# The last stage of a hybrid encoder: row factors of blocks 0 to 4 made two blocks later, and block 6's operand traced behind the first projection of block 7

## The chip, the cores and the metric

The kernel runs on one core of a Trainium2 chip. The metric is the device time of one execution in microseconds (us). A core has five engines that run side by side and meet through semaphores: TensorE (PE, matmuls; PEld is its weight load), VectorE (DVE), ScalarE (ACT), GpSimd (POOL) and SyncE (SP). Here nearly all DMAs are issued from SP's queue, one after the other.

## The reference

One layer of an encoder over 2048 + 256 rows of width 1024, in float32. The normalised input is projected once (`u @ w_in`), and the columns feed two mixers that run in both directions over the rows: gated linear attention with 4 heads (the GLA heads) and a Mamba-2 scan with 16 heads in 4 groups (the SSD groups). The outputs of both are normalised, joined and projected, and an embedding is added through a gate:

```
o   = rmsnorm(gla_forward + gla_backward, gla_onorm_g) * silu(z_gla)      # per head of 256
y   = rmsnorm((ssd_forward + ssd_backward + d*x) * silu(z_ssd), ssd_norm_g)
h   = x + concat(o, y) @ w_out
h   = h + sigmoid(h @ w_ple_gate) * rmsnorm(p @ w_ple_proj, ple_norm_g)
out = rmsnorm(h, final_norm_g)
```

The RMS norm of `o` needs one factor for each row and head: rsqrt of the mean of the squares over 256 columns.

## The kernel before, in words

The rows are cut into nine blocks of 256 (`NB = 9`, `T = 256`; block 8 is the second sequence). Everything is held with features on the partitions. Each float32 matmul is made of three in a rounded format: every operand is split into a high part (a copy by ACT, line 130) and a low part (a subtraction, line 126), and lines 195 to 197 multiply high by high, high by low and low by high.

**Stages.** Eight sections follow each other, a GLA head and an SSD group in turn (`s0` to `s7`). Each section walks over all blocks, odd ones from block 8 down to 0, projects, and runs the scan of one direction (`gla_first`, `ssd_first`, and their second halves, which wait in the list `queue`). The scan of the other direction (`second`, line 752) needs the section's stored updates and runs one section later, block by block; the list `carry` holds it until the next projection has been traced (`carried`), and `behind` then takes one entry out of `queue`. `second` ends in `emit`, which writes the gated output to `mixD` and, for a GLA head, the sums of squares of the rows to `ssD`.

**The last stage**, `output` (line 1243), begins when section 7 has been traced. Its first loop goes over the blocks from 8 down to 0 and multiplies the GLA half of `w_out`: four projections `foa` a block, 48 matmuls each, whose results are added to `x` (tile `fx`, line 1259) and stored. The other direction of section 7 runs inside this loop: at the end of each block the gate of the next `second` is made (`fz0zz` is the gate of block 0, `s7b0lo` the output tile of its `second`, and so on upwards), and it runs behind the first projection of the next block. The names of section 7's block 0, such as `s7b0fS`, `s7b0fU`, `s7b0fxh`, `s7b0y`, belong to its forward pass, which still runs while block 8 and 7 are multiplied; `s7b0lpf` is the first matmul group of its `second`, and `s7b0le`, `s7b1le` are row factors of `second` that SP loads (line 642).

**The operand of a block.** `gla_mix(b)` makes the operand of block b, called `fa8m` to `fa0m`: it loads the row factors `r` of the four heads from `rD[b]` (lines 818 to 821, four DMAs that copy one row to all partitions), loads `mixD[b]`, multiplies both on DVE (line 836) and splits the product (ACT, POOL). `fa6r` are the row factors of block 6. Two of the four pieces are made when `gla_mix` is called, the other two by `rest()`. The row factors of several blocks are made together by `gla_rstd` (line 840): it loads the sums of squares from `ssD`, takes Ln and Exp on ACT, and stores the result to `rD`. A call inside section 7 (`f1`) does blocks 5 to 8; the call in `output` (`f0`, tile `f0rc`) does blocks 0 to 4.

**What sets the order.** The code is traced in the order in which it is written, and a scheduler then places each engine's instructions by readiness and traced order; the order on every engine is fixed when the kernel is built. `tc.keep_in_program_order(i)` pins an instruction behind the one traced before it on its engine. A tile taken with `tmp(tag, ...)` gets one of the few buffers of its tag, and waits until one is free:

```python
bufs = {"t4k": 2, "dk": 6, "tm": 2, "zo": 4, "eb": 2, "mx": 7, ...}
r  = [tmp("zo", [P, 2, T], f"{nm}r{j}") for j in range(2)]      # gla_mix: row factors
zz = tmp("zo", [P, 2, T], nm + "zz")                            # gate_z: the gate
o  = tmp("zo", [P, 2, T], nm + "o")                             # second: its output
```

Of the kernel before, what the change touches and what calls it, by code (L numbers as in the profile page):

```python
# [19 lines left out]
NB = NBP + NBS  # L20
# [13 lines left out]
def hybrid(ctx, tc, xT, pT, wsec, wsmall, wlast, wproj, wgate, bgate, norm_g, gla_g,  # L34
# [89 lines left out]
    def split(raw, hi, lo, hi_eng, lo_eng):  # L124
        copy(hi_eng, hi, raw)
        lo_eng.tensor_tensor(lo, raw, hi.bitcast(F32), ALU.subtract)
# [58 lines left out]
    def load_u(b, name):  # L185
        def piece(n, hi, lo):
            for q, t in enumerate((hi, lo)):
                sy.dma_start(t.bitcast(F32), uD[b][n, q])
        return Operand(name, piece)
# [45 lines left out]
    def proj_f(w, u, name):  # L235

        ps = bank("pj", [P, 2, T], name)
        mm3_bank(ps, lambda f: wcols(w, f), lambda f: ucols(u))
        return ps
# [7 lines left out]
    def rstd(ss, r, n, e, pin=False):  # L247

        ln = sc.activation(r, ss, AF.Ln, bias=e[:, 0:1], scale=1.0 / n)  # L249
        if pin:  # L250
            tc.keep_in_program_order(ln)
        sc.activation(r, r, AF.Exp, scale=-0.5)  # L252
# [5 lines left out]
    with ExitStack() as mctx:  # L258
# [6 lines left out]
        def tmp(tag, shape, name, dt=F32):  # L265
            return mp.tile(shape, dt, name=name, tag=tag, bufs=bufs[tag])
# [142 lines left out]
        def carried(ps):  # L409

            while carry:
                carry.pop()()
            return ps

        def behind(n):

            if n:
                queue.pop(0)()
                if len(queue) > QMAX:
                    queue.pop(0)()  # L420
# [389 lines left out]
        def gate_z(pz, nm):  # L810

            zz = tmp("zo", [P, 2, T], nm + "zz")
            sc.activation(zz, pz, AF.Tanh, scale=0.5)  # L813
            ve.scalar_tensor_tensor(zz, zz, 1.0, pz, ALU.add, ALU.mult)
            return zz


        def rows(dst, src):

            for h in range(dst.shape[1]):  # L820
                sy.dma_start(dst[:, h, :], bass.AP(src.tensor, src.offset + h * T, [[0, P], [1, T]]))

        def mix_block(b, half, r, name, tags=()):

            raws = {}

            def piece(n, hi, lo):
                if n % 2 == 0:
                    r2 = upool.tile([P, 2, UK, T], F32, name=f"{name}_r{n}", tag="uraw", bufs=2)
                    sy.dma_start(r2, mixD[b][4 * half + n:4 * half + n + 2].rearrange("s p f t -> p s f t"))  # L830
                    raws[n], raws[n + 1] = r2[:, 0], r2[:, 1]
                raw = raws.pop(n)
                for k in range(UK):
                    kk = UK * n + k
                    g = g_gla[:, kk % 2:kk % 2 + 1] if half == 0 else g_ssd[:, kk:kk + 1]
                    ve.scalar_tensor_tensor(raw[:, k, :], raw[:, k, :], g, r(kk), ALU.mult, ALU.mult)
                split(raw, hi, lo, sc, po)
            return Operand(name, piece, tags)

        def gla_rstd(bs, nm):  # L840

            rc = tmp("lr", [NH * len(bs), T], nm + "rc")
            for j, b in enumerate(bs):
                sy.dma_start(rc[NH * j:NH * j + NH], ssD[b][0:NH, 0])
            rstd(rc, rc, 256.0, eps[0:NH * len(bs)], True)
            for j, b in enumerate(bs):
                sy.dma_start(rD[b], rc[NH * j:NH * j + NH])

        def gla_mix(b, nm):
            r = [tmp("zo", [P, 2, T], f"{nm}r{j}") for j in range(2)]  # L850
            for j in range(2):
                rows(r[j], rD[b][2 * j:2 * j + 2])
            tags = ("t4k", "t4k") if b < NB - 2 and b % 2 == 0 else ()
            return mix_block(b, 0, lambda k: r[k // 4][:, k // 2 % 2, :], nm + "m", tags)
# [24 lines left out]
        for i, s in enumerate(secs):  # L879
# [3 lines left out]
            for n, b in enumerate(s.order):  # L883
# [6 lines left out]
                elif not last:  # L890
# [3 lines left out]
                    u2 = load_u(b2, f"u{i}_{b2}")  # L894
                elif nxt is not None:
                    u2 = load_u(nxt.order[0], f"u{i}n")
                else:
                    u2 = gla_mix(NB - 1, "fa8")
                steps = need(i) if n == 0 or i == 0 else need(i)[1:] + need(i)[:1]
                for g, (wn, what) in enumerate(steps):  # L900
# [25 lines left out]
                    if i == 0:  # L926
                        if g == 0:
# [5 lines left out]
                            if not last:  # L933
                                u2 = prep_u(b + 1, xs, sums)
# [308 lines left out]
        def output(nm, wo, u, first):  # L1243

            s = secs[-1]
            wo2, wg = [], []
            for b in range(NB - 1, -1, -1):
                u2 = gla_mix(b - 1, f"{nm}a{b - 1}") if b else first_ssd()
                for m in range(4):
                    if m == (1 if b else 2):  # L1250
                        u2.rest()
                    x = tmp("mx" if m % 2 and b < NB - 2 else "dk", [P, 2, T], f"{nm}x{b}_{m}")
                    sy.dma_start(x, xT[b][:, 2 * m:2 * m + 2, :])
                    late = len(queue)
                    ps = carried(proj_f(wo[m], u, f"{nm}oa{b}_{m}"))
                    behind(late)
                    if first and b == NB - 1 and m == 1:
                        gla_rstd(range(5), "f0")
                    ve.tensor_tensor(x, ps, x, ALU.add)
                    sy.dma_start(h1D[b][:, 2 * m:2 * m + 2, :], x)  # L1260
                    if b == 2 and m == 1:
                        first_ssd = ssd_mix(0, f"{nm}b0")
                    elif b == 1 and m == 0:
                        first_ssd = first_ssd()
                    if b == 0:
                        wo2.append(load_w(wlast[4 + m], f"{nm}ob{m}"))
                u = u2
                if first:
                    bb = NB - 1 - b
                    z = tmp("mx", [P, 2, T], f"{nm}z{bb}")  # L1270
                    sy.dma_start(z, zD[bb])
                    carry.append(lambda a=(s, bb, gate_z(z, f"{nm}z{bb}")): second(*a))
            for b in range(NB):
                if b + 1 < NB:
                    u2 = ssd_mix(b + 1, f"{nm}b{b + 1}")
                else:
                    nxt = Last(0, wp, f"{nm}l0")
                for m in range(4):
                    if m == 2 and b + 1 < NB:
                        u2.rest()  # L1280
                    h = tmp("mx" if m % 2 else "dk", [P, 2, T], f"{nm}h{b}_{m}")
                    sy.dma_start(h, h1D[b][:, 2 * m:2 * m + 2, :])
                    late = len(queue)
                    ps = carried(proj_f(wo2[m], u, f"{nm}ob{b}_{m}"))
                    behind(late)
                    ve.tensor_tensor(h, ps, h, ALU.add)
                    sy.dma_start(hD[b][:, 2 * m:2 * m + 2, :], h)
                    if m == 1 and b + 1 < NB:
                        u2 = u2()()
                    if b == NB - 1:  # L1290
                        nxt.embed(m)
                        if m == 2:
                            nxt.load()
                        wg.append(load_w(wlast[8 + m], f"{nm}g{m}"))
                if b == NB - 3:
                    wp = [[tmp("xr" if q == 0 else "t4k", [P, 2, 512], f"{nm}wp{q}{j}", F32R) for j in range(2)]
                          for q in range(2)]
                    for j in range(2):
                        raw = upool.tile([P, 2, 512], F32, name=f"{nm}wpr{j}", tag="uraw", bufs=2)
                        sy.dma_start(raw, wproj[:, :, 512 * j:512 * j + 512])  # L1300
                        split(raw, wp[0][j], wp[1][j], sc, ve)
                u = u2
            before = None
            for b in range(NB):
                blk, nxt = nxt, None
                for m in range(4 if b + 1 < NB else 3):
                    ps = proj_f(wg[m], blk.uh, f"{nm}pg{b}_{m}")
                    if m == 0:
                        blk.norm()
                        if b + 1 < NB:  # L1310
                            nxt = Last(b + 1, wp, f"{nm}l{b + 1}")
                    blk.gate(m, ps)
                    for j in ((0, 1), (2,), (3,), ())[m]:
                        if nxt:
                            nxt.embed(j)
                    if m == 1:
                        if before:
                            before.store()
                        if nxt:
                            nxt.load()  # L1320
                before = blk
            before.finish(wg[3])
# [90 lines left out]
```

## Time and profile before

| what | value |
|---|---|
| median of 3 runs (lowest to highest) | 2452.09 us (2450.26 to 2455.7) |
| profiled execution: time, span | 2457.73 us, 2456.0 us |
| mean granted clock of TensorE | 0.992 |
| busy: PE, PEld, DVE, ACT, POOL | 97%, 96%, 67%, 51%, 19% of the span |
| `foa` in the last stage: first matmul on block 8, last on block 3 | 1707.8 us, 1882.4 us |

The profiled execution is one run with the hardware profiler on; its span reaches from the first to the last instruction. Engines work side by side, so a busy share says little alone: what counts is on which engine the end depends in a given stretch, and what that engine waits for. The granted clock is the share of full speed at which TensorE ran; 1.00 is 2.4 GHz and 0.50 is 1.2 GHz.

### The profile page before, as it was taken

To read this page: it belongs to the slowest core of one execution; us is meant where nothing else is said; L and a number is where in the kernel's file an instruction comes from. 1 tells how busy PE (TensorE), PEld (TensorE's weight loads), DVE (VectorE), ACT (ScalarE), POOL (GpSimd) and SP (SyncE) were. 2 spreads that over 40 slices of the span, in tenths; PEclk is the share of its full clock that TensorE was granted. 3 is DMA by queue.
4 is the path that set the end of the run, shared out by engine and by line. 5 is a ranking of instruction groups with operands and counts; after the bars stand their busy time and mean duration, and the time that the engine had idled before them with its cause. 6 is when DMAs were issued, how large, how long until landed. Compare 5 with 4: busy or idle time off the path is not lost. (4 is left out here: it accounts for less than half of the span.)

```text
span 2456.0 us, 50794 instructions
## 1 busy us (share of the span) xinstructions
PE 2393.6 (97%) x19736; PEld 2347.9 (96%) x19736; DVE 1642.3 (67%) x3572; ACT 1249.8 (51%) x2513; POOL 462.6 (19%) x519
## 2 busy tenths in 40 slices
PE   7999999999999999999999999999899999999997
PEld 7999899999999999999999999999899999999997
DVE  8887578965558895456888555689753543556665
ACT  5565455744445574444566444456421332356776
POOL 3221000033300004330001332000164532300000
PEclk9999999999999999999999999999999999999999
DMA  6545555654565564465566446545676665522221
GB/s 238 175 150 175 182 174 180 204 162 149 186 189 168 190 214 139 161 200 163 184 188 192 150 149 209 175 151 183 206 238 190 220 201 172 164 94 78 78 78 62
DMA packets 295586, 415.00 MB, mean 169 GB/s; under 512 B 33020, under 2 KB 140328, under 8 KB 295336
## 3 DMA queue, kind: packets, MB, share of 16 engines
q1 hardware_dynamic: 295048, 411.14, 52.6%
q8 instruction: 157, 2.57, 0.4%
q14 instruction: 93, 0.76, 0.1%
q10 hardware_dynamic: 288, 0.52, 0.1%
HBM read 319.21 MB, written 92.35 MB: 168 GB/s over the span
## 5 line engine op out<-in xcount | busy, mean ns | idle before, releaser
L195 PE MATMUL pz<-u_h,wh_n 128*128 128x256 f32 x896 | 257.7, 288 | 0.0
L197 PE MATMUL pz<-u_h,wl_n 128*128 128x256 f32 x896 | 256.6, 286 | 0.0
L196 PE MATMUL pz<-u_l,wh_n 128*128 128x256 f32 x896 | 254.7, 284 | 0.0
L197 PEld LDWEIGHTS pz<-u_h,wl_n 128*128 128x128 f32 x896 | 171.1, 191 | 2.3 <-issue 2.1
L195 PEld LDWEIGHTS pz<-u_h,wh_n 128*128 128x128 f32 x896 | 171.3, 191 | 1.2 <-issue 0.7
L196 PEld LDWEIGHTS pz<-u_l,wh_n 128*128 128x128 f32 x896 | 171.3, 191 | 0.4
L195 PE MATMUL pxb<-u_h,wh_n 128*128 128x256 f32 x512 | 148.3, 290 | 0.0
L196 PE MATMUL pxa<-u_l,wh_n 128*128 128x256 f32 x512 | 147.6, 288 | 0.0
L197 PE MATMUL pxb<-u_h,wl_n 128*128 128x256 f32 x512 | 146.0, 285 | 0.0
L195 PE MATMUL pxa<-u_h,wh_n 128*128 128x256 f32 x512 | 145.7, 285 | 0.0
L197 PE MATMUL pxa<-u_h,wl_n 128*128 128x256 f32 x512 | 145.0, 283 | 0.0
L196 PE MATMUL pxb<-u_l,wh_n 128*128 128x256 f32 x512 | 145.0, 283 | 0.0
L594 POOL MEMSET xr<- 128x4 f32 x16 | 1.4, 119 | 655.7 <-ACT z_1zz L813 330.6
L197 PE MATMUL pv<-wh_n,u_l 128*128 128x256 f32 x384 | 112.2, 292 | 0.0
L195 PE MATMUL pv<-wh_n,u_h 128*128 128x256 f32 x384 | 111.5, 290 | 0.0
L195 PE MATMUL pq<-u_h,wh_n 128*128 128x256 f32 x384 | 111.1, 289 | 0.0
L196 PE MATMUL pq<-u_l,wh_n 128*128 128x256 f32 x384 | 109.0, 284 | 0.0
L197 PE MATMUL pq<-u_h,wl_n 128*128 128x256 f32 x384 | 109.0, 284 | 0.0
L196 PE MATMUL pv<-wl_n,u_h 128*128 128x256 f32 x384 | 108.8, 283 | 0.0
L195 PEld LDWEIGHTS pxa<-u_h,wh_n 128*128 128x128 f32 x512 | 98.2, 192 | 0.7 <-issue 0.7
L196 PEld LDWEIGHTS pxa<-u_l,wh_n 128*128 128x128 f32 x512 | 98.2, 192 | 0.3
L197 PEld LDWEIGHTS pxa<-u_h,wl_n 128*128 128x128 f32 x512 | 98.2, 192 | 0.3
(5982 smaller groups left out, 9342.6 us busy)
## 6 DMA issues: line engine op xcount, KB each, us to landing
u_h<-uD SPq DMA_DIRECT2D x224, 256.0 KB
u_l<-uD SPq DMA_DIRECT2D x224, 256.0 KB
wr_n<-wsec SPq DMA_DIRECT2D x48, 512.0 KB
fx<-xT SPq DMA_DIRECT2D x36, 256.0 KB
h1D<-fx SPq DMA_DIRECT2D x36, 256.0 KB
fh<-h1D SPq DMA_DIRECT2D x36, 256.0 KB
hD<-fh SPq DMA_DIRECT2D x36, 256.0 KB
wr_oa<-wlast SPq DMA_DIRECT2D x8, 512.0 KB
```

The lines of the kernel that those rows point to most:

```text
L195: te.matmul(outs, lhsT=lh, rhs=rh, start=start and k == ks[0], stop=False, skip_group_check=True)
L196: te.matmul(outs, lhsT=lh, rhs=rl, start=False, stop=False, skip_group_check=True)
L197: te.matmul(outs, lhsT=ll, rhs=rh, start=False, stop=stop and k == ks[-1], skip_group_check=True)
L594: po.memset(xr[:, js, 0:2], 0.0)
```

## The change

The call of `gla_rstd` for blocks 0 to 4 moves from block 8 (behind its second projection) to block 6 (behind its first). And for block 7 alone `gla_mix(6)` is no longer traced ahead of the block's first projection but behind it, and behind what `carried` and `behind` trace there; the second half of that operand (`rest`) is traced ahead of the third projection and no longer ahead of the second.

```diff
             for b in range(NB - 1, -1, -1):
-                u2 = gla_mix(b - 1, f"{nm}a{b - 1}") if b else first_ssd()
+                late_mix = first and b == NB - 2
+                u2 = None if late_mix else gla_mix(b - 1, f"{nm}a{b - 1}") if b else first_ssd()
                 for m in range(4):
-                    if m == (1 if b else 2):
+                    if m == (2 if late_mix or not b else 1):
                         u2.rest()
                     x = tmp("mx" if m % 2 and b < NB - 2 else "dk", [P, 2, T], f"{nm}x{b}_{m}")
                     sy.dma_start(x, xT[b][:, 2 * m:2 * m + 2, :])
                     late = len(queue)
                     ps = carried(proj_f(wo[m], u, f"{nm}oa{b}_{m}"))
                     behind(late)
-                    if first and b == NB - 1 and m == 1:
+                    if first and b == NB - 3 and m == 0:
                         gla_rstd(range(5), "f0")
+                    if late_mix and m == 0:
+                        u2 = gla_mix(b - 1, f"{nm}a{b - 1}")
                     ve.tensor_tensor(x, ps, x, ALU.add)
```

## Rows read from the trace of the kernel before

**Rows 1.** The page: busy us, share of the span and instructions of each engine.
```profile
PE 2393.6 (97%) x19736; PEld 2347.9 (96%) x19736; DVE 1642.3 (67%) x3572; ACT 1249.8 (51%) x2513; POOL 462.6 (19%) x519
```

**Rows 2.** Waits of PE, whole span: for whom, us in total, times, longest.
```profile
PE p0ps L317 <- DVE p0s L303: 9.0, 1, 9.0
PE s7b0lpf L770 <- ACT s7b0fU L724: 4.5, 1, 4.5
```

**Rows 3.** Timeline of PE: start, us, instruction [idle before it <- what ended that].
```profile
1779.34 0.28 PE L195 MATMUL foa<-fa7m_h,wh_oa 128*128 128x256 f32 x1
1784.11 1.22 PE L770 MATMUL s7b0lpf<-s7b0qd,s7b0fU 128*128 128x128 f32 x4 [4.48 <-ACT s7b0fU L724]
...
1785.56 0.42 PE L195 MATMUL foa<-fa6m_h,wh_oa 128*128 128x256 f32 x1
...
1835.06 0.28 PE L195 MATMUL foa<-fa4m_h,wh_oa 128*128 128x256 f32 x1
```

**Rows 4.** Windows: from:to, us, then each engine's busy us, granted clock, DMA share, GB/s.
```profile
1721.30:1724.40 3.10, 0.06 (x2) 0.03 (x1) 3.10 (x10) 1.66 (x4) 0.00 (x0) 1.00 0.02 5
...
1727.00:1731.00 4.00, 3.74 (x17) 3.74 (x18) 4.00 (x6) 0.00 (x0) 1.63 (x2) 0.50 0.44 130
...
1779.50:1784.10 4.60, 0.12 (x2) 0.00 (x0) 4.60 (x9) 1.69 (x4) 3.58 (x4) 0.86 1.00 353
1784.10:1785.60 1.50, 1.49 (x7) 1.50 (x8) 1.47 (x3) 0.47 (x1) 1.50 (x2) 0.50 1.04 399
1785.60:1789.60 4.00, 4.00 (x20) 4.00 (x20) 2.22 (x4) 0.00 (x0) 3.68 (x6) 0.50 0.72 229
```

**Rows 5.** Timeline of ACT, 1764 to 1808 us.
```profile
1764.70 1.28 ACT L249 ACT_TABLE_LOAD   x1
1767.49 0.51 ACT L249 ACTIVATE f0rc<-f0rc,eps 20x256 f32<-20x256 f32 x1 [1.51 <-DMA f0rc<-ssD]
1767.90 0.57 ACT L666 ACTIVATE s7b0fxt<-s7b0fpxt 128x512 f32<-128x512 f32 x1
...
1771.79 0.63 ACT L813 ACTIVATE fz0zz<-fz 128x512 f32<-128x512 f32 x1 [1.07 <-DMA fz<-zD]
...
1783.67 0.38 ACT L724 ACTIVATE s7b0fU<-s7b0fpu 128x256 f32<-128x256 f32 x1 [0.30 <-DVE s7b0fS L458]
1783.95 0.62 ACT L813 ACTIVATE fz1zz<-fz 128x512 f32<-128x512 f32 x1
...
1807.20 0.63 ACT L792 ACTIVATE s7b1lo<-fz1zz 128x512 f32<-128x512 f32 x1 [4.91 <-POOL fz1zz L790]
```

**Rows 6.** Timeline of DVE, 1768 to 1811 us.
```profile
1768.51 1.29 DVE L673 TENSOR_TENSOR s7b0fxh<-s7b0fpxt,s7b0ftm 128x512 f32<-128x512 f32 x2 [2.92 <-ACT s7b0fxt L666]
...
1773.06 0.41 DVE L458 TENSOR_TENSOR s7b0fS<-s7b0fS,s7b0fpu 128x256 f32<-128x256 f32 x1
1777.02 1.67 DVE L836 SCALAR_TENSOR_TENSOR fa6m_r<-fa6m_r,g_gla,fa6r 128x256 f32<-128x256 f32 x4 [3.55 <-DMA fa6r<-rD]
...
1778.95 3.70 DVE L836 SCALAR_TENSOR_TENSOR fa6m_r<-fa6m_r,g_gla,fa6r 128x256 f32<-128x256 f32 x4
...
1805.84 4.83 DVE L836 SCALAR_TENSOR_TENSOR fa4m_r<-fa4m_r,g_gla,fa4r 128x256 f32<-128x256 f32 x4 [3.34 <-DMA fa4r<-rD]
```

**Rows 7.** Timeline of SP's DMA queue: start and us of the issue, 1770 to 1788 us.
```profile
1770.74 1.62 SPq L847 DMA_DIRECT2D rD<-f0rc  x5
1772.41 3.48 SPq L821 DMA_DIRECT2D fa6r<-rD  x4
...
1785.59 1.24 SPq L642 DMA_DIRECT2D s7b1le<-ebD  x2
1786.87 1.07 SPq L821 DMA_DIRECT2D fa5r<-rD  x2
```

**Rows 8.** Timeline of POOL, 1778 to 1820 us.
```profile
1778.71 2.87 POOL L126 TENSOR_TENSOR fa6m_l<-fa6m_r,fa6m_h 128x512 fp32r<-128x512 f32 x2 [31.00 <-ACT fa6m_h L130]
...
1786.35 0.79 POOL L778 COPY s7b0lo<-s7b0y 128x256 f32<-128x256 f32 x1 [0.32 <-DVE s7b0y L732]
...
1818.34 1.29 POOL L126 TENSOR_TENSOR fa4m<-fa4m_r,fa4m 128x512 fp32r<-128x512 f32 x1 [1.48 <-ACT fa4m L130]
```

## The prediction

> **What bounds the kernel now.** I read the page first: TensorE (PE) is busy nearly all of the span [rows 1], so only time in which PE stands still, or runs at half clock, can be won. The waits of PE over the whole execution come next. The second longest is a wait of 4.5 us for `s7b0fU`, and it lies in the last stage [rows 2]. In PE's timeline it is the gap between the matmul at 1779.34 and the four at 1784.11; block 6's operand `fa6m` is first multiplied at 1785.56 [rows 3]. The windows add a second cost. After the gap the granted clock is 0.50 from 1784.1 to 1789.6, the 1.2 GHz level: 5.5 us that do the work of 2.75. A gap of 3.1 us at 1721.3 was followed by half clock too [rows 4].
>
> Who is late? On ScalarE (ACT), `s7b0fU` stands behind four copies of `fa6m`; it ran at 1783.67, released by VectorE (DVE) [rows 5]. DVE had nothing to do for 3.55 us, until the row factors `fa6r` had landed at 1777.02, and worked on `fa6m_r` until about 1782.6, ahead of what `s7b0fU` waits for [rows 6]. On the DMA queue of SyncE (SP) the four loads of `fa6r` were issued from 1772.41, right behind the five stores of `f0rc`, which began when ACT had finished its Exp, at 1770.74 [rows 7]. `fa6r` does not need `f0rc` (those are the factors of blocks 0 to 4); it only stands behind it.
>
> **What the change does to this.** The ceiling: the wait gone and the half clock with it is 4.5 + 2.75 = 7.2 us of the 2457.73 us of the profiled execution. That execution is 5.6 us above the median of the runs, 2452.09; I take each difference from the median.
>
> *Row factors made later.* Two activations, the table loads around them and the ten small DMAs move from block 8 to block 6. Nothing is saved in work. On ACT the table load at 1764.70, the wait for the DMA and the Ln stand in front of `s7b0fxt`, which would follow at 1764.7 instead of 1767.90: 3.2 us [rows 5]. DVE waited 2.92 us for just that before `s7b0fxh` [rows 6], so 2.9 is what the chain of `s7b0` can gain here. It may also gain nothing: the next DVE step of that chain, `s7b0fS` at 1773.06, ran right behind `fz0zz`, whose tanh at 1771.79 waited 1.07 us for its own load of `fz` [rows 5, 6], and the change does not touch that load. So between 0 and 2.9 us, and I take the middle. In its new place Ln is pinned behind the square of `s7b1lo`, at 1807.20 before [rows 5]. The other engines are not charged for the ten DMAs: PE had no wait between 1785.56 and block 4's first matmul at 1835.06 [rows 3]. What that cover is worth is the last rival below.
>
> *Block 6's operand traced later.* The scaling of `fa6m_r` on DVE (a wait of 3.55, then 1.67 and 3.70 us [rows 6]) and the copies on ACT now come behind `second` of block 0. So `s7b0fU` no longer waits for them, and PE's gap at `s7b0lpf` goes. But what is late next is `fa6m` itself. Its row factors `fa6r` live in the pool `zo` of four buffers, and the trace shows how such loads wait. Those of `fa6r` were issued 0.6 us after the tanh that fills `fz0zz`, the `zo` tile traced before them. Those of `fa5r` came at 1786.87, 0.5 us after the first write of `s7b0lo` (1786.35) and behind `fz1zz` (1783.95), the two `zo` tiles traced before them [rows 5, 7, 8]. I read from this that the pool hands out buffers in the order of the trace. Before, the tile ahead of `fa6r` was `fz0zz`. Now it is `s7b0lo`, which is written only when the whole forward pass of block 0 has its sum `y`. The two loads of `s7b1le` are also traced ahead now; they were issued at 1785.59 for 1.24 us [rows 7].
>
> *The sum.* From `s7b0fS` at 1773.06 to `s7b0lo` at 1786.35 were 13.3 us, of which the wait for `fa6r` and the work on `fa6m_r` were 3.55 + 1.67 + 3.70 = 8.9 on DVE. Without them `s7b0lo` comes 4.4 us after `s7b0fS`: at 1777.4, or 1774.5 with the 2.9 us. Add 0.5 to the first issue of `fa6r`; 4.6 from that issue to the first use on DVE (1772.41 to 1777.02); and 3.1 from there to the first low part (1777.02 to 1780.1, half of the two that POOL began at 1778.71 [rows 8]). So `fa6m` is ready at 1785.6 or 1782.7, where it was first multiplied at 1785.56: a gain of 0 or 2.9 us, in the middle 1.4. PE itself would be through with block 7 at 1780.4 (the gap began 4.48 us before 1784.11, at 1779.63; the 1.45 us from 1784.11 to 1785.56 are 0.73 at full clock), so it stands for 2.3 to 5.2 us, in the range of the two gaps after which the clock was halved. I charge the half clock in full. Before, 1.45 of its 5.5 us passed before `fa6m`; now all of it falls on `fa6m`, 0.7 us more. 1.4 - 0.7 = 0.7 us faster, 2451.4. The bounds of this case: 2.2 us faster (2449.9) to 0.7 slower (2452.8); the other loads of that moment can widen it, since the 16 DMA engines were full from 1779.5 to 1784.1 (353 GB/s [rows 4]).
>
> The Trainium skill, "DMA: Bandwidth & Descriptors", section "Anatomy of one DMA", prices a transfer (fitted there for GpSimd's queue) at about 2.0 us plus its bytes by 436 GB/s: an estimate of 2.3 us for the 128 KB of one row. With the two issues ahead (some 1.7 us) that is 4.0 in place of 4.6, and the sum would be 2450.8; the trace has the longer time, and I keep it. The same page, section "Rules for kernel authors", says to issue a DMA early and wait for it late; that speaks against tracing the loads later, and the second case below is what the rule would want.
>
> **The rivals.** *(a) The wait is cured.* If the program's order still issues `fa6r` early enough, `fa6m` is there when PE is through with block 7, and 6.5 to 7.2 us are won: 2445 to 2446. For it: the five stores that stood ahead are gone, and buffers of block 7's factors are long free. It needs `s7b0lo` written 8.2 us before 1780.4, by 1772.2, against 1774.5 at the earliest of my sum. Part of it is enough: a gap too short to drop the clock already saves about 5.
>
> *(b) The row factors come too late for block 4 (slower).* Ln behind the square that ended at 1807.8 starts, with a table load of 1.28, at 1809.1. From Ln to the first store were 3.25 us (1767.49 to 1770.74), and I take 4.6 for the stores and 4.6 for the loads of `fa4r`. DVE could then begin `fa4m_r` at 1821.6 where it began at 1805.84, 15.8 later [rows 6]. The last part of `fa4m` ended at 1819.63 [rows 8]; 15.8 later is 1835.4. PE wants the first part at 1835.06, but that one comes early; the last serves the fourth dozen of matmuls, which at half clock take 0.20 each (20 in 4.0 us [rows 4]), so at least 0.10 at full clock, and is due 3.6 later at 1838.7. The margin is 3.3 us. If the chain slips by more, PE waits in block 4: a wait of 3.1 with 2.75 for the half clock makes 5.9, and 2457.3. Against it: the square comes earlier as soon as `s7b0` does.
>
> *(c) The change does nothing to the wait,* since loads, engines and PE keep their order: 2452.1.
>
> **How the numbers follow.** Forecast 0.48, (a) 0.26, (b) 0.18, (c) 0.08. The likeliest gives 2451.4, with a range of its own of 2449 to 2454. The range for 8 in 10 reaches to (a) and most of the way to (b): 2444.5 to 2456.5. A difference under 0.2% (4.9 us) can't be told from none: the three runs alone lie 5.4 us apart. Faster: (a), and a piece of the forecast, 0.28. Slower: (b), and a little for a schedule that shifts elsewhere, 0.2. The same: 0.52.
>
> **What would show it.** Right: no PE wait at `s7b0lpf`; a wait of some 2 to 5 us before the first matmul of `fa6m` that ends with its split; the loads of `fa6r` behind the first write of `s7b0lo` on SP; half clock after the wait; no PE wait at block 4. Wrong: `fa6r` issued well before `s7b0lo` is written, or PE passing from block 7 to block 6 without a stop (a); a wait for `fa4m` (b); or `s7b0fU` late again (c). The sum fails most easily at the 4.4 us and at the order in which SP issues the loads.

## The result, and the profile after

The change made the kernel slower: 2468.5 us, median of 6 runs (2465.27 to 2475.36), against 2454.52 us for the kernel before in 6 runs (2450.26 to 2455.7). The ratio is 1.0057, with a 95% interval of 1.0043 to 1.0071, some 14 us. The prediction was 2451.4 us with a range up to 2456.5, so it failed. The profiled execution took 2471.37 us with a span of 2469.6 us. All starts and waits below are read from one profiled execution of each kernel.

All of it lies in the loop that multiplies the first half of `w_out`. The windows show it from the first matmul on block 8 to the first on the second half (`fob`): from:to, us, then the busy us of PE, PEld, DVE, ACT and POOL, the granted clock, the DMA share and GB/s. First the kernel before:

```profile
1707.80:1956.20 248.40, 236.82 (x1922) 232.44 (x1921) 139.48 (x237) 69.10 (x127) 110.94 (x105) 0.97 0.67 211
```

and then the changed one:

```profile
1709.10:1971.50 262.40, 242.77 (x1922) 238.29 (x1921) 136.88 (x237) 69.56 (x127) 110.06 (x105) 0.94 0.64 199
```

The loop has grown by 14.0 us, from 248.4 to 262.4. PE stood still for 11.6 us before (248.40 less 236.82) and for 19.6 after: 8.0 more. The same 1922 matmuls took 242.77 in place of 236.82 us: 6.0 more, at a mean clock of 0.94 in place of 0.97. Waiting and the lower clock make the whole difference.

The waits of PE in this stretch, in the changed kernel (for whom, us, times, longest), where before had one of 4.5 us [rows 2] (both also wait 3.0 us for weights within block 8):

```profile
PE s7b1lpf L770 <- DVE s7b1lo L782: 5.9, 1, 5.9
PE foa L195 <- ACT fa6m_h L130: 4.6, 1, 4.6
PE s7b2lpf L770 <- DVE s7b2lo L782: 3.3, 1, 3.3
```

The old wait at `s7b0lpf` is gone, as forecast; the one at the first matmul of `fa6m` took its place, as forecast; two more came that the sum did not hold. PE's timeline, with the idle time in brackets:

```profile
1787.57 1.25 PE L195 MATMUL foa<-fa6m_h,wh_oa 128*128 128x256 f32 x4 [4.62 <-ACT fa6m_h L130]
...
1803.95 1.22 PE L770 MATMUL s7b1lpf<-s7b1qd,s7b1lS 128*128 128x128 f32 x4 [5.86 <-DVE s7b1lo L782]
...
1834.99 1.22 PE L770 MATMUL s7b2lpf<-s7b2qd,s7b2lS 128*128 128x128 f32 x4 [3.32 <-DVE s7b2lo L782]
```

And windows of the stretches behind those waits (the first three lines belong to a shorter wait, of 2.31 us at `s7b0fpxt`, told of at the end):

```profile
1765.30:1767.00 1.70, 1.70 (x8) 1.70 (x9) 1.70 (x3) 1.50 (x3) 0.00 (x0) 0.50 0.52 116
1767.00:1769.00 2.00, 2.00 (x12) 2.00 (x12) 2.00 (x5) 0.63 (x1) 0.00 (x0) 0.57 0.80 302
1769.00:1771.00 2.00, 2.00 (x20) 2.00 (x19) 0.50 (x1) 0.00 (x0) 0.00 (x0) 1.00 0.44 113
...
1787.50:1793.00 5.50, 5.32 (x24) 5.03 (x25) 5.50 (x7) 2.36 (x6) 5.41 (x5) 0.53 0.28 101
...
1804.00:1809.50 5.50, 5.50 (x26) 5.50 (x27) 5.35 (x5) 2.02 (x4) 5.50 (x5) 0.50 0.35 92
...
1835.00:1839.80 4.80, 4.80 (x22) 4.80 (x23) 2.95 (x3) 0.53 (x2) 4.56 (x6) 0.50 0.65 166
```

Each of the three waits is followed by about 5 us at half clock (granted clock 0.53, 0.50 and 0.50). The kernel before had paid this once between block 8 and the end of block 4, behind its wait of 4.48 us [rows 4].

Who is late, engine by engine. SP's queue (start and us of the issue):

```profile
1778.97 1.23 SPq L642 DMA_DIRECT2D s7b1le<-ebD  x2
1780.25 2.31 SPq L821 DMA_DIRECT2D fa6r<-rD  x4
...
1792.89 0.80 SPq L821 DMA_DIRECT2D fa5r<-rD  x2
...
1795.89 0.38 SPq L830 DMA_DIRECT2D fa5m_r<-mixD  x1
...
1820.98 1.63 SPq L847 DMA_DIRECT2D rD<-f0rc  x5
...
1824.18 1.75 SPq L821 DMA_DIRECT2D fa4r<-rD  x4
```

and what it waited for ahead of `fa5r` (us in total, times, longest):

```profile
SPq L821 <- DVE fa6m_r L836: 3.7, 1, 3.7
```

POOL's timeline, where block 0's `s7b0lo` is written and `fa6m` is split:

```profile
1779.23 0.40 POOL L778 COPY s7b0lo<-s7b0y 128x256 f32<-128x256 f32 x1
...
1787.59 1.28 POOL L126 TENSOR_TENSOR fa6m_l<-fa6m_r,fa6m_h 128x512 fp32r<-128x512 f32 x1 [2.67 <-ACT fa6m_h L130]
```

DVE's, with what it stood for in brackets:

```profile
1773.78 0.69 DVE L814 SCALAR_TENSOR_TENSOR fz0zz<-fz0zz,fz 128x512 f32<-128x512 f32 x1 [4.28 <-ACT fz0zz L813]
1774.39 0.41 DVE L458 TENSOR_TENSOR s7b0fS<-s7b0fS,s7b0fpu 128x256 f32<-128x256 f32 x1
...
1785.91 1.67 DVE L836 SCALAR_TENSOR_TENSOR fa6m_r<-fa6m_r,g_gla,fa6r 128x256 f32<-128x256 f32 x4 [3.80 <-DMA fa6r<-rD]
...
1788.10 4.76 DVE L836 SCALAR_TENSOR_TENSOR fa6m_r<-fa6m_r,g_gla,fa6r 128x256 f32<-128x256 f32 x4
...
1801.89 1.67 DVE L836 SCALAR_TENSOR_TENSOR fa5m_r<-fa5m_r,g_gla,fa5r 128x256 f32<-128x256 f32 x4 [7.88 <-DMA sqD<-s7b0lo]
1803.48 0.41 DVE L782 TENSOR_TENSOR s7b1lo<-s7b1lpf,s7b1le 128x256 f32<-128x256 f32 x1
...
1827.08 0.48 DVE L836 SCALAR_TENSOR_TENSOR fa4m_r<-fa4m_r,g_gla,fa4r 128x256 f32<-128x256 f32 x1 [9.60 <-DMA fa4r<-rD]
...
1834.53 0.41 DVE L782 TENSOR_TENSOR s7b2lo<-s7b2lpf,s7b2le 128x256 f32<-128x256 f32 x1
```

And ACT's, where Ln and Exp of the factors now stand:

```profile
1815.64 0.63 ACT L792 ACTIVATE s7b1lo<-fz1zz 128x512 f32<-128x512 f32 x1 [6.09 <-POOL fz1zz L790]
1816.29 1.28 ACT L249 ACT_TABLE_LOAD   x1
1817.58 0.51 ACT L249 ACTIVATE f0rc<-f0rc,eps 20x256 f32<-20x256 f32 x1
1818.11 1.28 ACT L252 ACT_TABLE_LOAD   x1
1819.40 0.42 ACT L252 ACTIVATE f0rc<-f0rc 20x256 f32<-20x256 f32 x1
```

Read them downwards. `fa6r` is issued 1.0 us behind the first write of `s7b0lo` and right behind `s7b1le`, so `fa6m_r` is scaled from 1785.91 and not from 1777.02 [rows 6]. `fa5r` then waits 3.7 us until DVE is through with `fa6m_r`, which frees the buffers of `fa6r` (1792.86; issued 1792.89; 1786.87 before [rows 7]). The loads of block 5's raw data stand behind `fa5r` on the queue and are issued from 1795.89. DVE, which takes its instructions in order, has nothing to do for 7.88 us, because the scaling of `fa5m_r` stands first; `s7b1lo` (line 782) stands behind it, and PE, in order too, stands at `s7b1lpf` until that has read its bank. Later the same picture once more: Ln runs behind the square of `s7b1lo`, the stores of `f0rc` follow at 1820.98, `fa4r` lands at 1827, and DVE has waited 9.60 us for it, with `s7b2lo` behind (1834.53).

### The profile page after: what moved, and what is told of

The parts are those of the page before. It is cut to its first block, busy times and chain, and to the rows that moved or that the text cites. A ratio compares the mean times of both kernels' runs of the same rounds, so it can differ in the third digit from the quotient of the medians.

```text
span 2469.6 us, 50790 instructions
## 1 busy us (share of the span) xinstructions
PE 2397.7 (97%) x19736; PEld 2350.8 (95%) x19736; DVE 1639.3 (66%) x3572; ACT 1250.9 (51%) x2513; POOL 461.3 (19%) x519
## 4 chain that ended last, share of the span: by engine, by line
PE 73%; DVE 11%; ACT 7%; DMA 6%; issue 2%; SPq 1%; POOL 0%; DVEq 0%; ACTq 0%; POOLq 0%
PE pz L197 4%; PE pz L195 4%; PE pz L196 4%; PE fob L195 3%; PE fob L196 3%; PE fob L197 3%; PE pxa L195 2%; PE pxa L197 2%; PE pxa L196 2%; PE pxb L197 2%; PE pxb L195 2%; PE pxb L196 2%; PE pv L197 2%; PE foa L196 2%; PE foa L197 2%; PE pv L195 2%
```

## The experiments

Two theories at first. **A**: each half of the change has its own wait; the late operand makes those at `fa6m` and `s7b1lpf`, because `fa6r` waits for its turn in the pool `zo`, and the late factors make the one at `s7b2lpf`. **B**: the factors' new place makes all three. All runs compute the whole output. The ratio is to the kernel before, run beside them, in 5 rounds (for the change, the runs of the section above); "loop" is measured as above, from the first matmul on block 8 to the first of `fob`, and several waits at one place are added up. Loop and waits come from one execution each, so a difference of a microsecond or two between them shows little; the ratios rest on all runs.

| kernel | ratio (95% interval) | loop, us | PE waits of 1.5 us or more behind block 8 in the loop, us |
|---|---|---|---|
| before | 1 | 248.4 | `s7b0lpf` 4.5, `fx` 1.5 |
| the change | 1.0057 (1.0043 to 1.0071) | 262.4 | `fa6m` 4.6, `s7b1lpf` 5.9, `s7b2lpf` 3.3, `s7b0fpxt` 2.3 |
| e1: factors only | 1.0021 (1.0009 to 1.0033) | 254.6 | `s7b0lpf` 1.7, `s7b1lpf` 2.8, `s7b2lpf` 5.0, `s7b0fpxt` 2.1 |
| e2: operand only | 1.0059 (1.0045 to 1.0073) | 265.2 | `fa6m` 8.0, `s7b1lpf` 5.7, `fx` 3.5 |
| e3: change, `fa6r` in its own buffers | 1.0016 (1.0005 to 1.0028) | 251.4 | `s7b1lpf` 2.8, `s7b2lpf` 4.4, `s7b0fpi` 1.7 |
| e4: before, `fa6r` in its own buffers | 1.0012 (1.0001 to 1.0024) | 247.8 | `fx` 3.2, `s7b0fpu` 2.0, `s7b1fpi` 1.7 |
| e5: before, factors of blocks 6 to 1 in their own | 1.0001 (0.9989 to 1.0013) | 246.6 | `s7b1lpf` 2.8 |
| e6: change, factors of blocks 6 to 1 in their own | 1.0015 (1.0001 to 1.0029) | 252.2 | `s7b2lpf` 7.3 |
| e7: factors of 0 to 4 one block later | 1.0000 (0.9987 to 1.0012) | 246.5 | `s7b0fpxt` 3.2, `s7b1lpf` 3.1, `s7b0lpf` 1.5 |
| e8: change, `s7b1lo` in its own buffer | 1.0043 (1.0028 to 1.0059) | 258.7 | `fa6m` 7.9, `s7b0fpxt` 3.0, `s7b2lpf` 2.8 |
| e9: second half of the operand only | 1.0000 (0.9992 to 1.0009) | 246.5 | `s7b0lpf` 3.1, `fx` 2.5 |
| e10: operand of block 6 earlier | 1.0007 (0.9993 to 1.0021) | 249.3 | `s7b0fpu` 2.8, `fx` 2.6, `s7b1lpf` 1.5, `s7b1fpu` 1.5 |
| e11: e7 and e5 together | 1.0006 (0.9995 to 1.0017) | 250.3 | `s7b2lpf` 7.7, `s7b0fpu` 1.9 |

**Each half alone.** e1 is the kernel before with

```diff
-                    if first and b == NB - 1 and m == 1:
+                    if first and b == NB - 3 and m == 0:
                         gla_rstd(range(5), "f0")
```

> Only the row factors of blocks 0 to 4 are made in block 6; gla_mix(6) stays ahead of block 7's first projection. Theory A (each half of the change has its own wait: the late operand makes the waits of PE at the first matmul of fa6m, 4.6 us, and at s7b1lpf, 5.9 us; the late factors make the one at s7b2lpf, 3.3 us): the loads of fa6r come right behind the tanh of fz0zz, PE's old wait at s7b0fU (4.5 us) shrinks to 2 us or less, no wait at fa6m or s7b1lpf, a wait of about 3 us at s7b2lpf with half clock behind it; 2447 to 2458 us. Rival B (the factors' new place, with its Ln and ten DMAs among block 6's work, makes all three waits): 2465 to 2470 us, with the wait at s7b1lpf.

e2 is the change with that line left at `b == NB - 1 and m == 1`.

> Only gla_mix(6) is traced behind block 7's first projection; the row factors of blocks 0 to 4 stay in block 8. Theory A: PE waits at the first matmul of fa6m (4 to 7 us, since the stores of f0rc stand on the queue too) and at s7b1lpf (5 to 6 us), not at s7b2lpf; some 9 us over before, 2461 to 2466 us. Rival B: no wait at s7b1lpf, 2450 to 2456 us.

e2 alone is as slow as the whole change, 1.0059 against 1.0057, and has the waits at `fa6m` and `s7b1lpf`; e1 has the one at `s7b2lpf` and costs 1.0021. So B falls: the operand makes the loss. A is right on the places, but not on all sizes. e2 lost more than the 9 us expected: at `fa6m` PE waits 8.0 and not 4.6. Here `fa6r` goes out 3.6 us behind the first write of `s7b0lo` (1779.13 to 1782.72) and not 1.0; that the stores of `f0rc`, still on the queue in front, cause this is not shown. And e1 has a wait of 2.8 at `s7b1lpf` that A did not have. The halves do not add up, 5 and 14 us making 14. One sign of A failed in e1. `fa6r` was to come right behind the tanh that fills `fz0zz`; it was issued 2.8 us ahead of it (SP, then ACT):

```profile
1770.58 1.85 SPq L821 DMA_DIRECT2D fa6r<-rD  x4
...
1773.39 0.63 ACT L813 ACTIVATE fz0zz<-fz 128x512 f32<-128x512 f32 x1 [5.13 <-DMA fz<-zD]
```

e7 has the same (1771.68 and 1774.25). So a load does not wait, while the kernel runs, for the first write of the tile traced ahead of it in `zo`. In the changed kernel, too, SP stood for nothing from 1778 to 1782: `fa6r` followed the loads in front of it. What a load does wait for is a buffer to come free, as `fa5r` did for 3.7 us. For `fa6r` the turn in `zo` must act through the place on SP's queue, which is fixed when the kernel is built.

In e2 the trace names what holds DVE in front of `s7b1lo`:

```profile
1804.69 1.67 DVE L836 SCALAR_TENSOR_TENSOR fa5m_r<-fa5m_r,g_gla,fa5r 128x256 f32<-128x256 f32 x4 [8.00 <-DMA fa5m_r<-mixD]
1806.28 0.41 DVE L782 TENSOR_TENSOR s7b1lo<-s7b1lpf,s7b1le 128x256 f32<-128x256 f32 x1
```

It is the load of block 5's raw data. On SP it stands behind the loads of `fa5r`, and these waited 3.4 us for block 6's scaling. In the changed kernel itself the store `sqD` is named, issued 1 us behind the first load of the raw data.

**Is it the turn in `zo`?** e3 is the change, e4 the kernel before, both with

```diff
-            r = [tmp("zo", [P, 2, T], f"{nm}r{j}") for j in range(2)]
+            r = [tmp("xc" if nm == "fa6" else "zo", [P, 2, T], f"{nm}r{j}") for j in range(2)]
```

(`xc` has two buffers. They are idle in the traced order between section 7 and block 2, but not in time: the kernel before loads `fb0r`, the sums of squares for the second half, into them at 1747.56 and 1797.53, and in e3 and e4 the first of these loads comes 18 and 19 us later from the loop's start.)

> The whole change, but the row factors of block 6 take two buffers of a pool that stands idle then (xc) and not of zo. Theory A (the loads of fa6r wait for their turn in zo behind s7b0lo, and everything behind fa6m inherits that): fa6r is issued before 1765 us, PE's waits at fa6m and at s7b1lpf are gone, the one at s7b2lpf (3.3 us and half clock) stays; 2449 to 2457 us. Rival C (zo has nothing to do with it: fa6m comes late because its work is traced later and the DMA queue is full): PE still waits 3 us or more at fa6m, 2463 to 2470 us.

> The kernel before, with the row factors of block 6 in the idle pool xc. Theory A: fa6r is issued long before the stores of f0rc, fa6m is scaled before s7b0fU is due, and PE's wait of 4.5 us at s7b0lpf goes with most of the half clock behind it; 5 to 7 us faster than before, 2447 to 2449 us. Rival C (the wait at s7b0fU comes from the order on DVE and ACT, not from the buffers): the wait stays over 3 us, 2453 to 2456 us.

In e3 SP issues `fa6r` in two pairs, 32 and 20 us earlier than in the change, although it is still traced behind the projection, and far ahead of the first write of `s7b0lo`, which POOL does at 1781.58:

```profile
1748.63 1.46 SPq L821 DMA_DIRECT2D fa6r<-rD  x2
...
1760.60 0.85 SPq L821 DMA_DIRECT2D fa6r<-rD  x2
```

The wait at `fa6m` is gone, and of the 14 us 4 are left, about what e1 costs alone. That shows the mechanism: not the traced place of the work as such, but the pool from which its row factors take their buffers; with other buffers they get another place on SP's queue. e4 cures the old wait at `s7b0lpf` just as well and gains nothing (1.0012). Here A was wrong on the value of the cure: up to block 5 the loop was ahead (99.0 us from the first matmul on block 8 to the first on block 5, at 1710.3 and 1809.3; 103.3 before), and at blocks 3 and 2 it lost it again. DVE in e4, then PE:

```profile
1880.35 0.88 DVE L836 SCALAR_TENSOR_TENSOR fa1m_r<-fa1m_r,g_gla,fa1r 128x256 f32<-128x256 f32 x2 [12.62 <-DMA fa1r<-rD]
...
1889.40 0.68 DVE L1259 TENSOR_TENSOR fx<-foa,fx 128x512 f32<-128x512 f32 x1
```

```profile
1890.13 0.39 PE L195 MATMUL foa<-fa2m_h,wh_oa 128*128 128x256 f32 x1 [1.98 <-DVE fx L1259]
```

DVE stands 12.62 us for `fa1r`, the additions `fx` that empty the projections' banks queue up behind it, and PE waits for one of them. This stop of DVE is not new; the kernel before has it too:

```profile
1879.51 0.88 DVE L836 SCALAR_TENSOR_TENSOR fa1m_r<-fa1m_r,g_gla,fa1r 128x256 f32<-128x256 f32 x2 [12.63 <-DMA fa1r<-rD]
```

Counted from the start of the loop it ends after 171.7 us there and after 170.0 in e4. PE came 4.3 us earlier to a stop that ends only 1.7 earlier.

**Is the rest of the loop paced by the same pool?** e5 (kernel before) and e6 (the change) take `xc` for all blocks from 6 to 1:

```diff
+            r = [tmp("xc" if nm[0] == "f" and 0 < b < NB - 2 else "zo", [P, 2, T], f"{nm}r{j}") for j in range(2)]
```

> The kernel before, with the row factors of blocks 6 to 1 in the idle pool xc. Theory A (the last stage is paced by the turn in zo; curing block 6 alone was given back at blocks 3 to 1, where DVE again sits on fa1m_r until fa1r lands): no wait of PE at s7b0lpf, none at the additions fx, and the loop from the first matmul on block 8 to the first on the second half of w_out takes 5 to 9 us less than before; 4 to 8 us faster in all. Rival D (the loop is paced by something else, the DMA queue or DVE, and what is won at one block is always given back later): within 3 us of before.

> The whole change, with the row factors of blocks 6 to 1 in the idle pool xc. Theory A: no wait at fa6m and none over 1 us at s7b1lpf; the wait at s7b2lpf stays if it comes from the late factors (fa4r waits for the stores of f0rc), 3 to 5 us with half clock behind it; 0 to 5 us slower than before. Rival D: the waits at fa6m and s7b1lpf stay, 10 us or more slower.

e5 did not get faster (1.0001), so A's claim that `zo` paces the whole loop falls, and rival D's forecast came: the loads of the raw data are the next to be late. The test is not a clean one, though: with the factors in `xc`, the loads of `fb0r` are issued only at 1871.64, from the loop's start 69 us later than the second of them in before, and what this costs was not measured. DVE's waits in e5 (for what, us, times, longest):

```profile
DVE fa3m_r L836 <- DMA fa3m_r<-mixD: 6.0, 1, 6.0
...
DVE fa1m_r L836 <- DMA fa1m_r<-mixD: 5.8, 1, 5.8
```

e6 has no wait left at `fa6m` or `s7b1lpf`, and the one at `s7b2lpf`, 7.3 us where A had 3 to 5, is the only one over 1.5 us left to explain its loss.

**When are the factors too late?** e7 is the kernel before with `gla_rstd` in block 7 (`b == NB - 2 and m == 0`).

> The kernel before, with the row factors of blocks 0 to 4 made one block later (block 7, behind the first projection) and nothing else moved. Theory A (the waits at s7b2lpf and s7b1lpf of the version two blocks later come from fa4r, which waits for f0rc): with one block the factors are there in time, no wait over 1 us at s7b2lpf; the wait at s7b0lpf is 0 to 3 us; 0 to 6 us faster than before. Rival E (any place behind block 8 is too late, because Ln is pinned behind the square of the last output tile): a wait of 3 us or more at s7b1lpf or s7b2lpf, 3 us or more slower than before.

No wait at `s7b2lpf`, and the old wait is down to 1.5 us: the price of e1 depends on the second block of delay. But `s7b0fpxt` and `s7b1lpf` have taken 3 us each. Rival E had the second, but with a loss of 3 us or more, and nobody the first; the time is that of before.

**The wait at `s7b1lpf`.** e8 is the change with `s7b1lo` in `xc`.

```diff
-            o = tmp("zo", [P, 2, T], nm + "o")
+            o = tmp("xc" if s.i == 7 and b == 1 else "zo", [P, 2, T], nm + "o")
```

> The whole change, with the output tile s7b1lo in the idle pool xc and not in zo. Theory A (PE's wait at s7b1lpf is that for a buffer: s7b1lo has to wait for the store of s7b0lo and so stands behind fa5m_r on DVE): the wait at s7b1lpf falls under 2 us, the one at fa6m stays at 4 to 6 us, the one at s7b2lpf stays; 5 to 10 us slower than before. Rival F (the wait at s7b1lpf comes from the late fa6m as such, whatever buffer its output takes): 5 us or more at s7b1lpf, 12 to 16 us slower than before.

The wait falls from 5.9 to 1.1 us: with its own buffer `s7b1lo` runs on DVE ahead of `fa5m_r` (its parts at 1799.42 and 1803.38):

```profile
1803.38 0.41 DVE L782 TENSOR_TENSOR s7b1lo<-s7b1lpf,s7b1le 128x256 f32<-128x256 f32 x1
1810.30 1.67 DVE L836 SCALAR_TENSOR_TENSOR fa5m_r<-fa5m_r,g_gla,fa5r 128x256 f32<-128x256 f32 x4 [6.51 <-DMA fa5m_r<-mixD]
```

So `s7b1lo` stands behind the late scaling only as long as it takes its buffer from `zo` as well. The wait at `fa6m` grew to 7.9, outside of what A allowed, and the saving is 3.4 us, less than the 4 to 9 that A gave.

**The third part of the diff, and its opposite.** e9 is the kernel before with `rest()` in block 7 at `m == 2`; e10 traces `gla_mix(6)` at the end of block 8, ahead of the gate `fz0zz`; e11 joins e7 and e5.

> The kernel before, with only the second half of block 6's operand (rest) traced ahead of the third projection of block 7 and not of the second. Theory A (what hurts is the turn of fa6r behind s7b0lo, which this does not change): within 3 us of before, and the loads of fa6r stay right behind the tanh of fz0zz. Rival G (the late second half is what costs): 5 us or more slower, with a wait of PE at fa6m.

> The opposite of the change: gla_mix(6) is traced ahead of the gate of block 0 (fz0zz), at the end of block 8; the factors of blocks 0 to 4 stay in block 8. Theory A (loads of row factors wait for their turn in zo): fa6r is issued before 1760 us and not behind the stores of f0rc, and PE's wait at s7b0lpf falls from 4.5 to under 2 us; in all 0 to 5 us faster, since part is given back behind block 3. Rival C (the place of fa6r in the trace does not decide): fa6r from about 1772 us as before, the wait of 4.5 us stays.

> A try at a faster version: the factors of blocks 0 to 4 in block 7, and the row factors of blocks 6 to 1 in the idle pool xc. Theory A with what the earlier runs gave: no wait over 3 us in the loop; the loop takes 244 to 247 us; in all 0 to 5 us faster than before. Rival D (whatever is won at block 7 is given back by the end of the loop): within 2 us of before.

e9: the late second half costs nothing (1.0000), with the first half in its old place. e10: `fa6r` goes out in front of the stores of `f0rc` (in pairs at 1741.63 and 1748.60, 31 and 24 us earlier than in before), and the wait at `s7b0lpf` is gone; moved up, the work gets an earlier place on the queue, as moved down it got a later one. But again nothing is won, 1.0007: `fx` and others take it back. e11, the try at a faster version, is no faster (1.0006): the wait at `s7b2lpf` is 7.7 us, where none over 3 was expected. No version here beats the kernel before.

## Why the prediction was wrong

*The factors made later, the first bound.* Right, at its lower end. `s7b0fxh` no longer waits for the table load and Ln, but `s7b0fS` still runs right behind `fz0zz` (1773.78 and 1774.39), whose tanh waits for its own load. The chain of `s7b0` gained nothing.

*The operand behind `s7b0lo`.* Right in the place, and near in every size. Forecast were 4.4 us from `s7b0fS` to `s7b0lo`, 0.5 to the loads, 4.6 to the first use and 3.1 to the first low part; measured 4.8 (1774.39 to 1779.23), 1.0, 5.7 (to 1785.91) and 3.0 (to 1788.87). PE waited 4.62 us at `fa6m` where 2.3 to 5.2 stood. From the start of the loop, `fa6m` was first multiplied after 77.8 us before and after 78.5 now: 0.7 later. e3 shows that the pool is the reason. The reading that led there was only half right, and the 0.5 us are in part luck. Before, `fa6r` was issued right behind the stores of `f0rc` [rows 7], so its 0.6 us behind the tanh could not tell a wait for the pool from a place in the queue; without these stores it went out ahead of the tanh (e1, e7), and in e2 it came 3.6 us behind the write of `s7b0lo`.

*The sum ended there, and that is the step that failed*: "The other engines are not charged for the ten DMAs: PE had no wait between 1785.56 and block 4's first matmul", and for the operand no charge at all behind its first matmul. I had priced how late `fa6m` is for PE, and not what a late `fa6m` holds. Its parts came 7.6 us later from the loop's start (1785.91 - 1709.1 = 76.8, against 1777.02 - 1707.8 = 69.2). DVE was through with them 8.9 us later (83.8, against 74.9), the factors gave their buffers back that much later, block 5's loads followed, and DVE, in order, let `s7b1lo` stand behind them. PE's wait at `s7b1lpf` and the half clock behind it were in no term: 5.86 us, and half of the 5.5 us behind it, are 8.6 of the 14.0. That `second` of block 1 needs DVE and a bank of PE in the middle of block 6 was in the code. The front part of the wait had moved as forecast (4.62 us, where before had 4.48); its tail is what cost. e2 has both without the late factors, and e3 loses the front and, with it, half of the wait at `s7b1lpf` (2.8 us are left).

*Rival (b).* Its chain was right in the order: Ln behind the square of `s7b1lo` (1815.64), table load, stores, loads of `fa4r`, DVE late at `fa4m_r` (1827.08; forecast 1821.6). Two sizes were wrong and partly cancel: the late operand put the square off by 7.1 us from the loop's start, and the stores and the loads took 3.2 and 2.9 us, not 4.6 each. The place where PE pays was wrong: not at the matmul on `fa4m`, where I had counted a margin of 3.3 us, but earlier, at `s7b2lpf`, whose `s7b2lo` stood behind `fa4m_r` on DVE. The price, 5.9 forecast, is close to the 5 us of e1, but by luck: e1 waits 5.0 us at `s7b2lpf` and 2.8 at `s7b1lpf`, and its old wait has shrunk from 4.5 to 1.7. So two of my cases came true at once, and I had given each a chance of its own, as if one excluded the other.

*Rival (a).* e4, e5 and e10 cured the old wait, and none was faster. None of these three cures got any of the 7.2 us of ceiling; in e4 the later blocks took it back. For the cost of a wait I had looked no further than its end.

The Trainium skill, "Trainium Kernel Development and Optimization", section "Best Practices", says that gaps that come again and again can mean that the on-chip buffers have run out. e3 agrees for the wait at `fa6m`, which went with two other buffers (4.6 us to none). e5 shows the limit of it: with the factors of six blocks out of `zo` the loop of the profiled execution was 1.8 us shorter, and the whole no faster.

What stays open: e1, e3, e5 and e7 have a wait of about 3 us at `s7b1lpf`, e6 and e11 one of over 7 at `s7b2lpf`, and e7 and e8 one of 3 at `s7b0fpxt`; which single buffer or load sets each of them was not tried.

## What to carry to other kernels

Work that is traced behind something else gets a later place in every queue, and a later turn in every pool of buffers, that it uses; before you move it, ask which tiles take buffers of that pool ahead of it, and behind which loads its own will then stand. Do not end the sum at the first instruction that is late: follow its buffers to the next load, and look what stands behind that load's first user on an engine that runs in order. And a wait is worth its own length only if the next wait behind it has slack; cure it in one run before counting on it.

## What was not expected of the hardware

The lower clock made 6.0 of the 14.0 us. After the waits of 4.62, 5.86 and 3.32 us the granted clock was 0.50 to 0.53 for about 5 us each time. A wait of only 2.31 us, at `s7b0fpxt` (it ended at 1765.26), was followed by half clock too: 0.50 until 1767, 0.57 in the next 2 us, and 1.00 from 1769 on. ACT loaded a table not only ahead of Ln but again between Ln and Exp of the same tile, 1.28 us each (1816.29 and 1818.11). Before, the second load stood at 1768.49, also between the two, ahead of another tile's Exp.
